# The beta and decay columns of a projection in plain fp32 on four column tiles, and an earlier first norm

## The chip, the cores and the metric

The kernel runs on one core of a Trainium2 chip. The metric is the device time of one execution in microseconds (us), as the median of several runs of the same program. Engine names are those of the profile: PE multiplies matrices, PEld is its weight load, DVE (VectorE), ACT (ScalarE) and POOL (GpSimd) work on vectors, SP (SyncE) issues most transfers.

## What is computed

One layer of a streaming encoder for 320 tokens: 256 of a new stream and 64 of a running one, 2048 channels each.

```python
h = rmsnorm(x, g_pre_mix)
p = h @ w_in                       # 2048 -> 6160 columns
a_out = conformer_conv(p[..., :c0], p[..., c0:c1], ...)          # channels of group A
b_out = gdn_mixer(p[..., c1:c2], p[..., c2:c3],                  # q, k, v and z of group B
                  p[..., c3:c4], p[..., c4:], ...)               # 8 columns for beta, 8 for the decay
x = x + rmsnorm(concat(a_out, b_out) @ w_out, g_post_mix)
x = x + rmsnorm(ffn(rmsnorm(x, g_pre_ffn)), g_post_ffn)

beta = sigmoid(b_raw)
g = -exp(a_log) * softplus(a_raw + dt_bias)
```

`rmsnorm` divides each token by the root of its mean square and multiplies by a weight per channel. The change concerns the last 16 columns of `w_in` (beta and decay, "the gate columns") and the root of the first norm.

## The kernel before

Tokens lie along the free axis (320 elements), channels along the 128 partitions in 16 blocks (`KB`). Each of the large products is done in three matmuls of a rounded type (fp32r): the weight is split into a high and a low part (`whi`, `wlo`, `split_w`, L213-219: a cast on ACT at L217, a subtraction on DVE at L218), and so is the input (`hi_t`, `lo_t`, that is x times the norm's weight g1). Then high by high (L233), high by low (L234) and low by high (L237) are summed in PSUM. The division by the root is done on the result, with `rb`, a row of roots broadcast to all partitions.

**Order at the start.** x and the first weights are loaded; 192 products of four blocks (`FIRST`) go to `ps_first` (L390-400) while ACT and DVE still split the rest. Beside them ACT squares x (`squares`) and DVE sums that into `ssum`, which has two halves of 320 tokens. Then come, in program order, the gate columns (`gate_products`, L307-312: 32 products into `psba`), then a block of `w_in` for v (`in_block(FIRST_V)`, 48 products into `psq`), with the job `first_norm` (L402-405) between them. That job sums `ssum` over partitions with products by a column of ones (`rstd`, L254-266: six matmuls into `pst`, DVE at L264, the power -0.5 on POOL at L265), waits for 36 more products, then turns the roots into a row over all partitions (`rstd_rows`, L268-273: three transposes into `psb`, L272) and ACT copies that to `rb` (L405).

**What sets the order.** `tick` (L148 on) counts the products of the large matmuls. At every 20th (`GAP`) it lets those jobs go one step on that are due; a job is a generator whose `yield` names how many products to wait for and how many PSUM slots it holds. What a job issues comes behind the product at which it was let go. The rest (weights ahead of use, `PRI_W`; urgent steps, `PRI_E`) follows from a priority. A weight goes through three slots `wst` for the loaded block (also used by a block of zeros `zt`) and three of `wsp` for the split. The blocks after `FIRST_V` follow `PLAN` (z blocks, heads h with `qkv_block` L621 on, convolution blocks c).

**The gates.** `gates` (L422-516) copies `psba` on ACT (L424, L425), multiplies by `rb` on DVE (L427, L428), transposes to tokens on partitions in three matmuls into `pst_ba` (L433), copies on ACT (L435) and adds high and low part on DVE (L436). A chain of small DVE operations for the softplus ends in `gt` (L462). 60 products (`LAG_GATE`) later come the sums over tokens, six matmuls into `psg` (L479, L480), then the exponentials and the decay products (`psd`). Between the root and `gt`, DVE also does the short convolutions of q, k and v (`cq`, L632: three steps for each block) and the subtractions of L218. Further on, the head's tail copies `kd` on ACT (L706), and the inverse of small matrices runs on tiles of PE smaller than 128 by 128 (L792, L815, L836).

Of the kernel before, what the change touches and what calls it, by code (L numbers as in the profile page):

```python
# [9 lines left out]
F32 = mybir.dt.float32  # L10
# [7 lines left out]
P = 128  # L18
# [82 lines left out]
def trunk_kernel(ctx, tc, ins, outs):  # L101
# [34 lines left out]
    def start(gen, wait, g=0, t=0):  # L136
        job = [dense[1] + wait, gen, g, t, []]
        jobs.append(job)
        return job
# [8 lines left out]
    def tick(mm):  # L148
        dense[0] = mm.ins
        dense[1] += 1  # L150
        if dense[1] % GAP == 0:
            g, t0, behind, due = 0, held_t[0], dense[0], []
            t = t0
            n0 = len(nc.cur_bb.bb.instructions)
            done = []
            for job in sorted(jobs, key=lambda j: j[0]):
                if job[0] <= dense[1] and g + job[2] <= 4 and t + job[3] <= 2:
                    g += job[2]
                    t += job[3]
                    due.append(job)  # L160
            for job in due:
                if not job[4]:
                    behind = advance(job, behind)
                    done.append(job)
            last_of = [i for x in (mybir.EngineType.Activation, mybir.EngineType.DVE)
                       if (i := newest(x, n0)) is not None]
            for job in due:
                if job[4] and job not in done:
                    with ExitStack() as e:
                        for i in last_of:  # L170
                            e.enter_context(tc.issue_after(i))
                        advance(job)
            held_t[0] = t - t0
            front = newest(mybir.EngineType.DVE, n0)
            for _ in range(min(pace[0], len(taps))):
                next_tap(front)
# [28 lines left out]
    def load_dma(src):  # L205
        w = wst.tile([P, HALF], F32, tag="w", name="w")
        dst = w[:, 0:src.free_size()]
        if len(src.shape) == 3:
            dst = dst.rearrange("p (a f) -> p a f", a=src.shape[1])
        nc.sync.dma_start(dst, src)  # L210
        return w

    def split_w(w, width, pool=None):  # L213
        pool = pool or wsp
        hi = pool.tile([P, HALF], F32R, tag="whi", name="whi")
        lo = pool.tile([P, HALF], F32R, tag="wlo", name="wlo")
        S.copy(hi[:, 0:width], w[:, 0:width])  # L217
        V.tensor_tensor(lo[:, 0:width], w[:, 0:width], hi[:, 0:width].bitcast(F32), ALU.subtract)  # L218
        return hi, lo

    def load_split(src, width, pool=None):
        with tc.high_priority(offset=boost[0]):
            return split_w(load_dma(src), width, pool)

    def block_matmul(ps, src, rhs, nks, final=True, first=True):
        nk = sum(nks)
        k0 = 0
        for nk_part in nks:
            hi, lo = load_split(src[:, k0 * P:(k0 + nk_part) * P], nk_part * P)
            for j in range(nk_part):  # L230
                xh, xl = rhs(k0 + j)
                wh = hi[:, j * P:(j + 1) * P]
                tick(PE.matmul(ps, wh, xh, start=(first and k0 + j == 0), stop=False))  # L233
                tick(PE.matmul(ps, wh, xl, start=False, stop=False))  # L234
            for j in range(nk_part):
                xh, xl = rhs(k0 + j)
                tick(PE.matmul(ps, lo[:, j * P:(j + 1) * P], xh, start=False, stop=(final and k0 + j == nk - 1)))  # L237
            k0 += nk_part
# [68 lines left out]
    def gate_products(wz):  # L307
        psba = ps_p.tile([P, 512], F32, tag="p", name="psba")
        for k in range(KB):
            tick(PE.matmul(psba[:, 0:T], wz[:, k, :], hi_t[k], start=(k == 0), stop=False))  # L310
            tick(PE.matmul(psba[:, 0:T], wz[:, k, :], lo_t[k], start=False, stop=(k == KB - 1)))
        return psba


# [1 line left out]
    with tc.tile_pool(name="xp", bufs=1) as xp:  # L316
# [9 lines left out]
        with tc.high_priority():  # L326
# [6 lines left out]
            nc.sync.dma_start(cst, ins["cst"][:, 0:NCST1])  # L333
            wba = xp.tile([P, KB, 16], F32, tag="wba", name="wba")
            nc.sync.dma_start(wba, ins["w_ba"])
        wbz = xp.tile([P, KB, P], F32R, tag="wbz", name="wbz")
        G.memset(wbz.bitcast(F32), 0.0)
        nc.sync.dma_start(par[:, NGV:NPAR], ins["par"][:, NGV:NPAR])
        nc.sync.dma_start(gpar[:, 0:8], ins["a_log"].partition_broadcast(P))
        nc.sync.dma_start(gpar[:, 8:16], ins["dt_bias"].partition_broadcast(P))  # L340
# [1 line left out]
        with tc.high_priority(offset=PRI_E):  # L342
            keep_warm(psw, NWARM)

            last = {}

            def then(eng, fn, *args, **kw):
                with ExitStack() as e:
                    if eng in last:
                        e.enter_context(tc.issue_after(last[eng].ins))  # L350
                    last[eng] = fn(*args, **kw)

            def split_part(hi, lo, w, o, n):
                then(S, S.copy, hi[:, o:o + n], w[:, o:o + n])
                then(V, V.tensor_tensor, lo[:, o:o + n], w[:, o:o + n], hi[:, o:o + n].bitcast(F32), ALU.subtract)

            ssum = xp.tile([P, 2, T], F32, tag="ssum", name="ssum")

            def squares(k):
                x = xt[k // 4][:, k % 4:k % 4 + 2, :]  # L360
                if k == 0:
                    then(S, S.activation, ssum, x, AF.Square)
                else:
                    sq = xp.tile([P, 2, T], F32, tag="sq", bufs=2, name="sq")
                    then(S, S.activation, sq, x, AF.Square)
                    then(V, V.tensor_tensor, ssum, ssum, sq, ALU.add)

            for k in range(KB):
                x = xt[k // 4][:, k % 4, :]
                g = pv("g1", k)  # L370
                then(S, S.activation, hi_t[k], x, AF.Identity, scale=g)
                then(V, V.scalar_tensor_tensor, lo_t[k], x, g, hi_t[k].bitcast(F32), ALU.mult, ALU.subtract)
                if k % 2 == 0:
                    pre.append((wsp.tile([P, HALF], F32R, tag="whi", name="whi"), wsp.tile([P, HALF], F32R, tag="wlo", name="wlo")))
                if k < 4:
                    split_part(*pre[-1], wg[k // 2], (k % 2) * FW, FW)
                elif k % 2:
                    split_part(*pre[-1], wg[k // 2], 0, 2 * FW)
                if k % 2 and k >= 5:
                    squares(k - 5)  # L380
            then(S, S.copy, wbz[:, :, 0:16], wba)
            then(V, V.tensor_tensor, wbz[:, :, 16:32], wba, wbz[:, :, 0:16].bitcast(F32), ALU.subtract)
            for k in (KB - 4, KB - 2):
                squares(k)
        for i, b in enumerate(FIRST):
            pool = (ps_t, ps_g)[i // 2]
            ready[b] = pool.tile([P, 512], F32, tag=pool.name[-1], name="ps_first")
# [12 lines left out]
                                tick(PE.matmul(ps, w, xl, start=False, stop=False))  # L400

        def first_norm():  # L402
            rr, _ = rstd([ssum[:, 0, :], ssum[:, 1, :]])
            yield 36, 1, 0
            S.copy(rb, rstd_rows(rr)[0])  # L405

        job = start(first_norm(), 24, 1)
        psba = gate_products(wbz)
        ready[FIRST_V] = in_block(FIRST_V, "psq")
        finish(job)  # L410
    boost[0] = PRI_W
    cb = pa.enter_context(tc.tile_pool(name="cb", bufs=2, reuse_waits="tile"))
    gd = pa.enter_context(tc.tile_pool(name="gd", bufs=2, reuse_waits="tile"))
# [2 lines left out]


    gate = {}
    cst2 = act.tile([P, NCST - NCST1], F32, tag="bl7", name="cst2")
    nc.sync.dma_start(cst2, ins["cst"][:, NCST1:NCST])  # L420

    def gates():  # L422
        baT = cb.tile([32, 3, P], F32, tag="un", bufs=1, name="baT").rearrange("p c f -> p (c f)")
        S.copy(baT[:, 0:T], psba[0:32, 0:T])  # L424
        S.copy(baT[:, T:T + TS], psba[0:32, TP:T])  # L425
        yield 1, 0, 0
        V.tensor_tensor(baT[:, 0:T], baT[:, 0:T], rb[0:32, :], ALU.mult)  # L427
        V.tensor_tensor(baT[:, T:T + TS], baT[:, T:T + TS], rb[0:32, TP:T], ALU.mult)  # L428
        ba = const.tile([P, 3, 16], F32, tag="ba", name="ba")
        yield LAG_WAIT, 0, 1  # L430
        pst = ps_t.tile([P, 512], F32, tag="t", name="pst_ba")
        for c in range(3):
            PE.transpose(pst[:, c * 32:(c + 1) * 32], baT[:, c * P:(c + 1) * P], cv("ident", 32, 32))  # L433
        ps3 = pst[:, 0:96].rearrange("p (c f) -> p c f", c=3)
        S.copy(ba, ps3[:, :, 0:16])  # L435
        V.tensor_tensor(ba, ba, ps3[:, :, 16:32], ALU.add)  # L436
        beta = const.tile([P, 3, NH], F32, tag="beta", name="beta")
        S.activation(beta, ba[:, :, 0:8], AF.Tanh, scale=0.5)
        G.tensor_scalar(beta, beta, 0.5, 0.5, ALU.mult, ALU.add)
# [91 lines left out]
    def conv_block(b):  # L531
        psg_ = in_block(8 + b, "psgate")
        ub = ubufs[b % 3]
        with tc.high_priority(offset=PRI_E):
            sg = cb.tile([P, T], F32, tag="sg", bufs=1, name="sg")
            V.tensor_tensor(sg, psg_[:, 0:T], rb, ALU.mult)
            S.activation(sg, sg, AF.Tanh, scale=0.5)
        psv = in_block(b, "psv")
        if b > 2:
            finish_conv(b - 3)  # L540
        with tc.high_priority(offset=PRI_E):
# [782 lines left out]
```

## Time and profile before

| | |
|---|---|
| median of 3 runs | 1489.62 us (1489.47 to 1491.08) |
| the profiled execution | 1489.37 us |
| its span in the profile | 1487.6 us |
| outside the span | 1.8 us |
| granted PE clock | 1.00 |
| first gate product, first `psq` product | 33.96 us, 40.00 us |
| `rb` copied | 45.81 us |
| first `psg` product | 69.05 us |

Times inside the profile are microseconds from the start of its span. A row of the timeline has the start, the duration and the engine, then the line, the operation and its operands (written before read); in square brackets stands the idle time of the engine just before it, and what ended that. A PE product of 320 tokens is listed with 0.31 us or so, but the next one starts 0.15 us behind it: products overlap in the pipeline, so costs are taken from the distance of starts. A plain fp32 product leaves two records, an fp32r product one.

### The profile page before, as it was taken

How to read it: one execution, taken by the hardware profiler on the slowest of the kernel's cores; microseconds unless marked ns; L12 is line 12 of the kernel's file. 1: busy time of each engine (PE TensorE's matmuls, PEld its weight loads, DVE VectorE, ACT ScalarE, POOL GpSimd, SP SyncE). 2: the span in 40 equal slices, each digit the busy share in tenths (PEclk: the TensorE clock that was granted, in tenths of full speed). 3: DMA queues.
4: the chain of work that ended last, by engine and by line, in shares of the span. 5: the costliest groups of instructions: out<-in, count | busy, mean ns of one | idle time of the engine just before them, and what ended most of it. 6: DMA issues, size and time to landing. Idle time of an engine off the chain costs nothing.

```text
span 1487.6 us, 27264 instructions
## 1 busy us (share of the span) xinstructions
PE 1478.6 (99%) x10610; PEld 1458.2 (98%) x10610; DVE 996.6 (67%) x1816; ACT 730.8 (49%) x1331; POOL 230.5 (15%) x390
## 2 busy tenths in 40 slices
PE   9999999999999999999999999999999999999998
PEld 8999999999999989999999999999999999999997
DVE  6779888888989678756336665545666545656554
ACT  7674556655454656544334444334444334444453
POOL 0111101021010000322002322002232001223101
PEclk9999999999999999999999999999999999999999
DMA  8435453544444734444554444554444455444453
GB/s 294 140 115 167 158 151 110 147 156 138 129 122 145 238 128 146 146 156 121 153 168 155 145 154 135 143 162 158 156 143 147 136 148 168 153 156 143 136 148 119
DMA packets 98281, 224.22 MB, mean 151 GB/s; under 512 B 18792, under 2 KB 39528, under 8 KB 98152
## 3 DMA queue, kind: packets, MB, share of 16 engines
q1 hardware_dynamic: 98008, 222.45, 47.8%
q8 instruction: 83, 1.36, 0.4%
q14 instruction: 46, 0.38, 0.1%
q10 hardware_dynamic: 144, 0.03, 0.0%
HBM read 215.33 MB, written 7.12 MB: 150 GB/s over the span
## 4 chain that ended last, share of the span: by engine, by line
PE 95%; ACT 2%; DVE 1%; issue 1%; DMA 0%; POOL 0%; DVEq 0%; ACTq 0%; POOLq 0%
PE psu L237 13%; PE psu L234 13%; PE psu L233 13%; PE psdn L233 7%; PE psdn L234 7%; PE psdn L237 7%; PE psq L233 3%; PE psq L234 3%; PE psq L237 3%; PE psm L237 2%; PE psm L233 2%; PE psm L234 2%; PE psu L1117 1%; PE psv L233 1%; PE psgate L233 1%; PE ps_first L398 1%
## 5 line engine op out<-in xcount | busy, mean ns | idle before, releaser
L217 ACT CAST whi<-w 128x1024 fp32r<-128x1024 f32 (+2 forms) x440 | 412.6, 940 | 488.5 <-PE psu L234 169.7
L218 DVE TENSOR_TENSOR wlo<-w,whi 128x1024 fp32r<-128x1024 f32 (+2 forms) x440 | 477.2, 1085 | 191.4 <-ACT whi L217 123.9
L233 PE MATMUL psu<-hi,whi 128*128 128x320 f32 x1344 | 397.0, 309 | 0.0
L234 PE MATMUL psu<-lo,whi 128*128 128x320 f32 x1344 | 396.9, 309 | 0.0
L234 PEld LDWEIGHTS psu<-lo,whi 128*128 128x128 f32 x1344 | 252.3, 188 | 0.0
L233 PEld LDWEIGHTS psu<-hi,whi 128*128 128x128 f32 x1344 | 252.2, 188 | 0.0
L237 PE MATMUL psu<-hi,wlo 128*128 128x320 f32 x1344 | 224.4, 309 | 0.0
L237 PEld LDWEIGHTS psu<-hi,wlo 128*128 128x128 f32 x1344 | 204.1, 188 | 0.0
L234 PE MATMUL psdn<-gl,whi 128*128 128x320 f32 x660 | 195.9, 310 | 0.0
L1150 POOL COPY nffn<-fbuf 128x2 f32<-128x2 f32 x88 | 99.5, 1131 | 586.7 <-DVE fbuf L1148 583.5
L1148 DVE TENSOR_TENSOR fbuf<-psu,rb 128x256 f32<-128x256 f32 x88 | 37.4, 424 | 169.1 <-PE psu L237 169.0
L233 PE MATMUL psdn<-gh,whi 128*128 128x320 f32 x480 | 142.8, 309 | 0.0
L234 PEld LDWEIGHTS psdn<-gl,whi 128*128 128x128 f32 x660 | 123.9, 188 | 0.3
L233 PE MATMUL psq<-hh,whi 128*128 128x320 f32 x352 | 106.0, 314 | 0.0
L234 PE MATMUL psq<-hl,whi 128*128 128x320 f32 x352 | 104.1, 309 | 0.0
L233 PEld LDWEIGHTS psdn<-gh,whi 128*128 128x128 f32 x480 | 90.1, 188 | 0.0
L237 PE MATMUL psdn<-gh,wlo 128*128 128x320 f32 x480 | 89.9, 309 | 0.0
L237 PEld LDWEIGHTS psdn<-gh,wlo 128*128 128x128 f32 x480 | 75.3, 188 | 0.0
L233 PEld LDWEIGHTS psq<-hh,whi 128*128 128x128 f32 x352 | 66.1, 188 | 0.4
L234 PEld LDWEIGHTS psq<-hl,whi 128*128 128x128 f32 x352 | 66.1, 188 | 0.2
L563 DVE SCALAR_TENSOR_TENSOR cvt<-ub,par,cvt 128x320 f32<-128x320 f32 x120 | 65.3, 545 | 0.1
L1193 DVE TENSOR_TENSOR y<-y,psdn 128x320 f32<-128x320 f32 x45 | 22.0, 488 | 58.7 <-PE psdn L237 58.7
(356 smaller groups left out, 2485.2 us busy)
## 6 DMA issues: line engine op xcount, KB each, us to landing
w<-in_w_up SPq DMA_DIRECT2D x176, 512.0 KB
w<-in_w_in SPq DMA_DIRECT2D x88, 512.0 KB
w<-in_w_down SPq DMA_DIRECT2D x64, 384.0 KB
w<-in_w_down SPq DMA_DIRECT2D x64, 320.0 KB
w<-in_w_out SPq DMA_DIRECT2D x32, 320.0 KB
w<-in_w_out SPq DMA_DIRECT2D x16, 384.0 KB
w<-in_w_first SPq DMA_DIRECT2D x6, 512.0 KB
wtp<-wsp SPq DMA_DIRECT2D x4, 640.0 KB
```

Source lines behind the costliest of these rows:

```text
L217: S.copy(hi[:, 0:width], w[:, 0:width])
L218: V.tensor_tensor(lo[:, 0:width], w[:, 0:width], hi[:, 0:width].bitcast(F32), ALU.subtract)
L233: tick(PE.matmul(ps, wh, xh, start=(first and k0 + j == 0), stop=False))
L234: tick(PE.matmul(ps, wh, xl, start=False, stop=False))
L237: tick(PE.matmul(ps, lo[:, j * P:(j + 1) * P], xh, start=False, stop=(final and k0 + j == nk - 1)))
L398: tick(PE.matmul(ps, w, xh, start=(k == 0 and wt is hi), stop=(k == KB - 1 and wt is lo)))
L563: return lambda: V.scalar_tensor_tensor(acc, x, w, acc, ALU.mult, ALU.add)
L1117: PE.matmul(pss[i][:, 0:T], wt[:, o:o + P], x, start=(k == 0 and n == 0), stop=(k == KB - 1 and n == 2))
L1148: V.tensor_tensor(buf[:, 2:258], psu[:, 0:TP], rb2[:, 0:TP], ALU.mult)
L1150: G.tensor_copy(nffn[:, b, 0, :], buf[:, 256:258])
L1193: V.tensor_tensor(y[:, n, :], y[:, n, :], psd[:, 0:T], ALU.add)
```

## The change

- The gate columns are no longer split. `wbz` holds 32 columns for each block of channels, 16 of them w times g1 (one DVE multiplication), the rest zero; 16 matmuls in plain fp32 take it with x itself. Block k writes to the partitions from 32 (k mod 4) of `psba`: four column tiles, each with the sum of four blocks. Sixteen ticks follow behind the last one.
- DVE adds the two halves of `ssum`, so three matmuls make the sum for the first norm. `first_norm` is due at once, waits 16 products instead of 36, and its second step has a high priority. The next product of a large matmul is issued behind the last `psb` transpose (`pin`).
- The ACT casts of weights are issued behind the copy of `rb` (`hold`) until the first convolution block clears that.
- In `gates` all 128 partitions are copied and multiplied by `rb`; three matmuls by `pick` (four identities of 16 below one another, made by a DVE reduction) add the four tiles and transpose at once. The DVE addition is gone.

```diff
     def split_w(w, width, pool=None):
...
-        S.copy(hi[:, 0:width], w[:, 0:width])
+        with ExitStack() as e:
+            for i in hold:
+                e.enter_context(tc.issue_after(i))
+            S.copy(hi[:, 0:width], w[:, 0:width])
...
-                tick(PE.matmul(ps, wh, xh, start=(first and k0 + j == 0), stop=False))
+                with ExitStack() as e:
+                    if pin:
+                        e.enter_context(tc.issue_after(pin.pop()))
+                    mm = PE.matmul(ps, wh, xh, start=(first and k0 + j == 0), stop=False)
+                tick(mm)
...
         for k in range(KB):
-            tick(PE.matmul(psba[:, 0:T], wz[:, k, :], hi_t[k], start=(k == 0), stop=False))
-            tick(PE.matmul(psba[:, 0:T], wz[:, k, :], lo_t[k], start=False, stop=(k == KB - 1)))
+            i = 32 * (k % 4)
+            mm = PE.matmul(psba[i:i + 32, 0:T], wz[:, k, :], xt[k // 4][:, k % 4, :], start=(k < 4), stop=(k >= KB - 4),
+                           skip_group_check=True)
+        for _ in range(16):
+            tick(mm)
...
-        wbz = xp.tile([P, KB, P], F32R, tag="wbz", name="wbz")
-        G.memset(wbz.bitcast(F32), 0.0)
+        wbz = xp.tile([P, KB, 32], F32, tag="wbz", name="wbz")
+        G.memset(wbz, 0.0)
...
-            then(S, S.copy, wbz[:, :, 0:16], wba)
-            then(V, V.tensor_tensor, wbz[:, :, 16:32], wba, wbz[:, :, 0:16].bitcast(F32), ALU.subtract)
+            then(V, V.tensor_tensor, wbz[:, :, 0:16], wba, pv("g1").unsqueeze(2).to_broadcast((P, KB, 16)), ALU.mult)
             for k in (KB - 4, KB - 2):
                 squares(k)
+            then(V, V.tensor_tensor, ssum[:, 0, :], ssum[:, 0, :], ssum[:, 1, :], ALU.add)
...
-            rr, _ = rstd([ssum[:, 0, :], ssum[:, 1, :]])
-            yield 36, 1, 0
-            S.copy(rb, rstd_rows(rr)[0])
+            rr, _ = rstd([ssum[:, 0, :]])
+            yield 16, 1, 0
+            with tc.high_priority(offset=PRI_E):
+                rows, mm = rstd_rows(rr)
+                pin.append(mm.ins)
+                spread.append(S.copy(rb, rows).ins)
...
-        job = start(first_norm(), 24, 1)
+        spread = []
+        job = start(first_norm(), 0, 1)
...
+    hold.extend(spread)
...
-        baT = cb.tile([32, 3, P], F32, tag="un", bufs=1, name="baT").rearrange("p c f -> p (c f)")
-        S.copy(baT[:, 0:T], psba[0:32, 0:T])
-        S.copy(baT[:, T:T + TS], psba[0:32, TP:T])
+        baT = cb.tile([P, 3, P], F32, tag="un", bufs=1, name="baT").rearrange("p c f -> p (c f)")
+        S.copy(baT[:, 0:T], psba[:, 0:T])
+        S.copy(baT[:, T:T + TS], psba[:, TP:T])
+        V.tensor_reduce(pick, cv("ident").rearrange("p (a j) -> p j a", j=32)[:, 0:16, :], AX.X, ALU.add)
...
-            PE.transpose(pst[:, c * 32:(c + 1) * 32], baT[:, c * P:(c + 1) * P], cv("ident", 32, 32))
-        ps3 = pst[:, 0:96].rearrange("p (c f) -> p c f", c=3)
-        S.copy(ba, ps3[:, :, 0:16])
-        V.tensor_tensor(ba, ba, ps3[:, :, 16:32], ALU.add)
+            PE.matmul(pst[:, c * 16:(c + 1) * 16], baT[:, c * P:(c + 1) * P], pick, start=True, stop=True)
+        S.copy(ba, pst[:, 0:48].rearrange("p (c f) -> p c f", c=3))
...
         psv = in_block(b, "psv")
+        hold.clear()
```

On PE before, this is the end of the gate columns (`psba`), where the sum for the first norm (`pst`) stands among them; `hh` and `hl` are the high and low part of the input, and `psq` is the block for v.

```order
L310 MATMUL psba<-hh_106,wbz 128x320
L311 MATMUL psba<-hl_122,wbz 128x320
L259 MATMUL pst<-cst,ssum 128x1 x6
L310 MATMUL psba<-hh_107,wbz 128x320
L311 MATMUL psba<-hl_123,wbz 128x320
L310 MATMUL psba<-hh_108,wbz 128x320
L311 MATMUL psba<-hl_124,wbz 128x320
L233 MATMUL psq<-hh_93,whi 128x320
L234 MATMUL psq<-hl_109,whi 128x320
```

On PE in the changed kernel, this is the same place; `xt` is the input as it was loaded.

```order
L322 MATMUL psba<-xt_129,wbz 32x320 x4
L322 MATMUL psba<-xt_130,wbz 32x320 x4
L322 MATMUL psba<-xt_131,wbz 32x320 x4
L322 MATMUL psba<-xt_132,wbz 32x320 x4
L270 MATMUL pst<-cst,ssum 128x1 x3
L243 MATMUL psq<-hh_93,whi 128x320
L245 MATMUL psq<-hl_109,whi 128x320
L243 MATMUL psq<-hh_94,whi 128x320
```

The 16 products stand together with the three of the sum behind them; the transposes into `psb` stand behind 12 products of `psq`, where before they stand behind 36. From the `psb` transposes to the `psg` products it is 139 products of 320 tokens, before 154; from the `pst_ba` matmuls to `psg` it is 79, before 114.

On ACT before, these are the casts of weights (`whi`) around the copy of `rb`; the other copies set up buffers and fetch `psba`.

```order
L217 CAST whi<-w 128x1024 x2
L625 COPY qb_593<-par 128x3
L625 COPY qb_594<-par 128x3
L546 COPY ub_587<-par 128x30
L546 COPY ub_588<-par 128x30
L546 COPY ub_589<-par 128x30
L424 COPY baT<-psba 32x320
L425 COPY baT<-psba 32x64
L474 CAST strict<-cst 128x128
L217 CAST whi<-w 128x1024
L405 COPY rb<-psb 128x320
L217 CAST whi<-w 128x1024
```

On ACT in the changed kernel, this is the same place.

```order
L222 CAST whi<-w 128x1024
L645 COPY qb_575<-par 128x3
L645 COPY qb_576<-par 128x3
L566 COPY ub_569<-par 128x30
L566 COPY ub_570<-par 128x30
L566 COPY ub_571<-par 128x30
L444 COPY baT<-psba 128x320
L445 COPY baT<-psba 128x64
L493 CAST strict<-cst 128x128
L422 COPY rb<-psb 128x320
L222 CAST whi<-w 128x1024
L979 ACT_TABLE_LOAD
```

The third and the fourth cast of a weight from `w_in` stood ahead of the copy of `rb`; now the third stands directly behind it, and the fourth behind the first activations that use `rb`.

More of the change, by code (lines that the diff above doesn't have):

```diff
@@ L211, in load_dma @@
         return w
+    hold = []
     def split_w(w, width, pool=None):
@@ L223, in load_split @@
             return split_w(load_dma(src), width, pool)
+    pin = []
     def block_matmul(ps, src, rhs, nks, final=True, first=True):
@@ L418, in trunk_kernel @@
     gate = {}
+    pick = const.tile([P, 16], F32, tag="pick", name="pick")
     cst2 = act.tile([P, NCST - NCST1], F32, tag="bl7", name="cst2")
@@ L422, in gates @@
     def gates():
-        baT = cb.tile([32, 3, P], F32, tag="un", bufs=1, name="baT").rearrange("p c f -> p (c f)")
-        S.copy(baT[:, 0:T], psba[0:32, 0:T])
-        S.copy(baT[:, T:T + TS], psba[0:32, TP:T])
+        baT = cb.tile([P, 3, P], F32, tag="un", bufs=1, name="baT").rearrange("p c f -> p (c f)")
+        S.copy(baT[:, 0:T], psba[:, 0:T])
+        S.copy(baT[:, T:T + TS], psba[:, TP:T])
+        V.tensor_reduce(pick, cv("ident").rearrange("p (a j) -> p j a", j=32)[:, 0:16, :], AX.X, ALU.add)
         yield 1, 0, 0
-        V.tensor_tensor(baT[:, 0:T], baT[:, 0:T], rb[0:32, :], ALU.mult)
-        V.tensor_tensor(baT[:, T:T + TS], baT[:, T:T + TS], rb[0:32, TP:T], ALU.mult)
+        V.tensor_tensor(baT[:, 0:T], baT[:, 0:T], rb, ALU.mult)
+        V.tensor_tensor(baT[:, T:T + TS], baT[:, T:T + TS], rb[:, TP:T], ALU.mult)
         ba = const.tile([P, 3, 16], F32, tag="ba", name="ba")
```

## The prediction

> **What bounds the kernel now.** I read the page first, then the waits of PE, then the timeline of each engine over the first 72 us, where the change acts.
>
> ```profile
> span 1487.6 us, 27264 instructions
> PE 1478.6 (99%) x10610; PEld 1458.2 (98%) x10610; DVE 996.6 (67%) x1816; ACT 730.8 (49%) x1331; POOL 230.5 (15%) x390
> PEclk9999999999999999999999999999999999999999
> ```
>
> PE works 99% of the span, at full clock in every slice. So time goes with PE's own work: what is taken off PE is won, unless PE then waits. The waits of PE say where it does (releaser: total us, times, longest):
>
> ```profile
> PE psm L1063 <- DVE wlo L218: 1.1, 2, 0.8
> PE psz L233 <- ACT whi L217: 0.6, 1, 0.6
> PE psg L479 <- DVE gt L462: 0.2, 1, 0.2
> ```
>
> Two of them lie behind the change: `psg` waits for the gates' chain on DVE, `psz` for a cast on ACT. The third is far on, where the order on PE is the same again. The stretch that is changed, on PE's timeline:
>
> ```profile
> 33.96 0.31 PE L310 MATMUL psba<-hh,wbz 128*128 128x320 f32 x1
> ...
> 37.92 0.31 PE L311 MATMUL psba<-hl,wbz 128*128 128x320 f32 x1
> 38.06 1.40 PE L259 MATMUL pst<-cst,ssum 128*128 128x1 f32 x12
> 39.32 0.39 PE L310 MATMUL psba<-hh,wbz 128*128 128x320 f32 x1
> ```
>
> From the first to the 28th gate product it is 3.96 us over 27 steps: 0.147 us each. The sum for the norm holds PE from 38.06 to 39.32, 1.26 us for 12 records: 0.105 each. Nothing waits here.
>
> **The change, part by part.** *Removed from PE.* 32 products of 0.147 are -4.69 us. Three of six sum matmuls, six records of 0.105, are -0.63. The addition of the halves that replaces them is half of a row such as this one (640 elements in 0.82, so an estimated 0.45 on DVE), and the gate products cover it, since PE needs the sum only at their end:
>
> ```profile
> 31.18 0.82 DVE L351 TENSOR_TENSOR ssum<-ssum,sq 128x640 f32<-128x640 f32 x1
> ```
>
> The multiplication by g1 takes the place of a DVE subtraction of the same size; the ACT cast and most of the memset go. All lie beside the first 192 products: nothing.
>
> *Added to PE: 16 plain fp32 products of 320 tokens.* Plain fp32 at this length stands at the kernel's end; smaller tiles of PE stand in the inverse:
>
> ```profile
> 1476.92 2.33 PE L1239 MATMUL fin<-y,cst 128*128 128x320 f32 x8
> 1479.09 0.43 PE L1160 MATMUL fin<-x,cst 128*128 128x320 f32 x1
> ```
>
> ```profile
> 171.82 0.31 PE L234 MATMUL psgate<-hl,whi 128*128 128x320 f32 x1
> 172.06 0.50 PE L815 MATMUL pz<-wtp,np 32*32 32x32 f32 x20
> 172.50 0.42 PE L233 MATMUL psgate<-hh,whi 128*128 128x320 f32 x1
> 186.29 0.68 PE L836 MATMUL px<-wtp,zq 64*64 64x64 f32 x8
> 160.10 0.53 PE L792 MATMUL pz<-wtp,np 32*32 32x16 f32 x40
> ```
>
> ```profile
> L815 PE MATMUL pz<-wtp,np x80: 191/191/212, 172.1 to 392.8; 32*32 32x32 f32 x80
> L836 PE MATMUL px<-wtp,zq x32: 218/218/267, 186.3 to 407.1; 64*64 64x64 f32 x32
> L792 PE MATMUL pz<-wtp,np x160: 177/178/198, 160.1 to 382.1; 32*32 32x16 f32 x160
> ```
>
> Four products leave eight records in 2.17 us (1476.92 to 1479.09): 0.271 a record, two a product. One after another, 32 records are 8.67 us: dearer than what goes. It hangs on the tiles running side by side. L836 uses one tile at a time: (0.68 - 0.218)/7 = 66 ns a record of 64 columns, half of it 33 for 32. L815 alternates between two tiles: (0.50 - 0.191)/19 = 16.3 ns. So two tiles give 2.0 of 2. L792 takes four tiles in turn, with 16 columns: (0.53 - 0.178)/39 = 9.0 ns where one tile would take 66/4 = 16.5, or 1.8 of 4. Records that short may be held by their issue, not by their columns; 9 ns for each would be no limit to records of 271 ns. No row has four tiles on the same 128 rows. Bounds: 2.17 us four at a time, 8.67 none. I take four at a time, because nothing in the pair of rows makes tiles cost each other anything.
>
> Into and out of the tiles it costs a little: 172.06 - 171.82 is 0.24, 0.09 over a normal step; the group lasts 0.44 (to 172.50), its 20 records 0.33: 0.11. Together 0.20, so 2.35 us. [...]
>
> *The root.* Its chain before:
>
> ```profile
> 39.80 0.87 POOL L265 TENSOR_TENSOR rr<-rr,nhalf 128x3 f32<-128x3 f32 x1 [10.47 <-DVE rr L264]
> 45.29 0.49 PE L272 MATMUL psb<-cst,rr 128*128 128x128 f32 x3
> 45.81 0.43 ACT L405 COPY rb<-psb 128x320 f32<-128x320 f32 x1 [2.21 <-PE psb L272]
> ```
>
> From the end of the sum on PE (39.32) over a step on DVE to the end of POOL (40.67) it is 1.35 us. After: gate products end at 36.3, the sum at 36.94, the root at 38.29; 12 products of `psq` end at 36.94 + 1.76 = 38.70. So 0.4 us of cover, where before it was 4.6 us. If that is gone, the transposes wait by as much, and with them all of PE (the next product is pinned behind them). `rb` then is copied from 39.2 to 39.65, 6.2 us earlier than before; relative to PE's products by 24 of them.
>
> *The held casts.* Before, on ACT and DVE:
>
> ```profile
> 36.20 1.05 ACT L217 CAST whi<-w 128x1024 fp32r<-128x1024 f32 x1 [5.36 <-DMA w<-in_w_in]
> ...
> 46.40 1.05 ACT L217 CAST whi<-w 128x1024 fp32r<-128x1024 f32 x1 [0.16 <-PE psq L234]
> ...
> 50.89 1.04 ACT L217 CAST whi<-w 128x1024 fp32r<-128x1024 f32 x1
> 37.28 1.23 DVE L218 TENSOR_TENSOR wlo<-w,whi 128x1024 fp32r<-128x1024 f32 x1 [4.15 <-ACT whi L217]
> ```
>
> The third cast moves from 36.20 to 39.7-40.75. PE needs it behind 48 products of `psq`, at 36.94 + 7.06 + 0.24 = 44.2: cover 3.4 us. On ACT the table load, zT, qb and cq now stand ahead of the fourth cast. They took from 47.45 to 50.89, 3.44 us: the cast ends at 45.3, needed 24 products on, at 47.75, cover 2.5; its subtraction, behind the short convolutions on DVE, has some 2.0. On SP, transfers queue behind the subtraction that frees their slot, 4.7 us later than before, for products ten and more us away. So nothing; without cover a late cast costs its lateness.
>
> *The gates' chain.* PE's way:
>
> ```profile
> 51.34 0.31 PE L234 MATMUL psq<-hl,whi 128*128 128x320 f32 x1
> 51.58 0.37 PE L433 MATMUL pst_ba<-cst,baT 32*128 32x32 f32 x3
> 51.87 0.41 PE L233 MATMUL psq<-hh,whi 128*128 128x320 f32 x1
> 69.05 0.40 PE L479 MATMUL psg<-gt,cst 128*128 128x16 f32 x2 [0.19 <-DVE gt L462]
> 69.29 0.37 PE L480 MATMUL psg<-gt,cst 128*128 128x8 f32 x2
> ```
>
> The three transposes cost 0.53 - 0.15 = 0.38. The three plain fp32 matmuls have six records: 0.63 by the sum's row, 0.72 by two `psg` records in 0.24. I take +0.25. `psg` stands 154 products behind `psb` before, 139 after: 15 x 0.147 = 2.20 us less time for DVE, 1.95 with those 0.25. What DVE loses in that stretch is three `cq` steps and the addition; its busy time there (PE, PEld, DVE, ACT, POOL) shows how full it is:
>
> ```profile
> 46.27:68.99 22.72, 22.59 (x154) 22.09 (x152) 20.53 (x50) 18.35 (x43) 1.89 (x3) 1.00 0.41 140
> 50.37 2.87 DVE L632 SCALAR_TENSOR_TENSOR cq<-qb,par,cq 128x320 f32<-128x320 f32 x6 [0.76 <-ACT cq L630]
> 53.56 0.20 DVE L436 TENSOR_TENSOR ba<-ba,pst_ba 128x48 f32<-128x48 f32 x1
> ```
>
> Three `cq` of 2.87/6 = 0.48 are 1.43, the addition 0.11 to the next start: 1.54. So `psg` comes 1.95 earlier and `gt` 1.54: the wait grows from 0.2 to some 0.6. DVE idles 22.72 - 20.53 = 2.19 us of the stretch, part of which can be used up. I take +0.3; bounds -0.35 (wait gone) and +2.5 (none of DVE's time is won).
>
> *The cast before psz.*
>
> ```profile
> 102.62 0.37 ACT L706 ACTIVATE kd<-tkq,sc 128x128 f32<-128x128 f32 x1 [1.14 <-POOL sc L699]
> 107.02 0.37 ACT L706 ACTIVATE kd<-tkq,sc 128x128 f32<-128x128 f32 x1 [0.69 <-POOL sc L699]
> 109.59 2.93 ACT L217 CAST whi<-w 128x1024 fp32r<-128x1024 f32 x3
> 110.68 0.41 PE L233 MATMUL psz<-hh,whi 128*128 128x320 f32 x1 [0.58 <-ACT whi L217]
> ```
>
> The second tail's transposes, which start the `kd` copies ahead of that cast, now stand 40 products ahead of `psz`, not 56: 2.35 us less slack. Against it, work of ACT moves ahead of them and fills its waits (1.14 + 0.69), and PE's copies come sooner. I take 0, bounds -0.74 (the whole gap ahead of it) and +2.35.
>
> *Sum:* -4.69 - 0.63 + 2.35 + 0.25 + 0.3 + 0 = -2.42 us. The profiled execution took 1489.37 (span 1487.6 and 1.8 around it), 0.25 under the median of 1489.62. So 1486.95 by the one, **1487.2 us** by the other, -0.16%: under the 0.2% (2.98 us) that a measurement of this kernel can tell from no change.
>
> **The rivals.** *Two at a time.* If the two records of a product stay together on their tile and products start in order, only the second record of one meets the first of the next. Then 16 x 0.271 + 0.20 = 4.54 us, the sum is -0.23, and the time 1489.4. For it speaks L792 with 1.8 of 4; against it L815, whose 2.0 of 2 such an order allows as well, though no more. *One after another, slower.* If tiles on the same 128 rows share what feeds those rows, 32 records take 8.67 + 0.20: +4.10 us, 1493.7. Each tile in L815 has rows of its own, so the trace doesn't exclude it. It decides from 7.7 us on for the 16 products (2.98 + 4.69 + 0.63 - 0.25 - 0.3). *The gates' chain late.* DVE wins none of its time, `psg` waits 2.5 us: -0.22, 1489.4. Against it the three steps less ahead of `gt`; for it that subtractions of weights, held back to the same stretch, stand among the chain's steps.
>
> **How the numbers follow.** Four at a time 0.66, two 0.17, one 0.11, the late chain 0.06. Within the first, both waits gone (-0.65 and -0.74 on the sum) gives 1485.8; a little under that, 1485.5, is the low end. The high end, 1490.6, takes in the second and fourth with the upper half of the `psz` bound; outside are the third and the tails. Faster by over 0.2% (under 1486.6) is some two fifths of the likeliest case: 0.28. Slower (over 1492.6): the third and a sum of late chain and late cast, 0.13. Within: 0.59.
>
> **What would show it.** Right: the gate products' records start some 0.068 us apart and the stage lasts 2.3 to 2.8 us; `psb` starts near 38.7 and `rb` is copied near 39.2; `psg` waits for `gt` by 0.3 to 0.8; no wait of PE for a weight between 37 and 60 us. Wrong: a gate stage of 4.5 or 8.9 us; a wait at `psb` for POOL; waits for `wlo` ahead of 60 us; `psz` waiting over 1 us.

## The result and the profile after

The changed kernel takes 1492.85 us (median of 21 runs, 1490.36 to 1495.6), the kernel before 1489.62 (21 runs, 1488.54 to 1491.08): a ratio of 1.0021, 95% interval 1.0015 to 1.0027. It is slower by some 3.2 us, where 2.4 us less were forecast. The profiled execution has a span of 1491.2 us, 3.6 over that of before. The page's head:

```profile
span 1491.2 us, 27264 instructions
PE 1478.5 (99%) x10607; PEld 1455.1 (98%) x10607; DVE 997.7 (67%) x1817; ACT 730.6 (49%) x1330; POOL 234.1 (16%) x390
```

PE is busy for as long as before, although work of 3 us was taken from it. Either a product takes longer somewhere, or PE stands idle: here it is both. The main waits of PE that were not there before or have grown:

```profile
PE pvns L913 <- DVE rhs L905: 1.1, 1, 1.1
PE px L842 <- ACT zq L837: 0.9, 1, 0.9
PE psg L498 <- DVE gt L481: 0.9, 1, 0.9
PE psz L243 <- ACT whi L222: 0.8, 1, 0.8
PE px L818 <- ACT zh L813: 0.5, 1, 0.5
```

`px`, `pvns` and their like belong to the heads' inverse and delta rule, 80 us and more behind the lines that were edited. To see where the time goes, the start of the same product was taken from the PE records of each trace, at the first product of a block, in us from the start of that trace's span. The rows name the block and its start in the kernel before; the columns are differences to that (the kernels of the later columns are the experiments below):

```
block   before   changed  16 ticks  psg     32 ticks  32 t.,   32 t.,     32 t.,
        at us    kernel   less      later             zeros    exp first  psg later
psq      40.00   -2.80    +0.05     -2.83   -2.73     -2.84    -3.18      -3.20
psgate   70.78   +0.17    +0.02     -2.56   +3.32     +2.27    -2.99      -4.74
psq      86.25   -0.30    +0.01     -3.03   +3.58     +1.79    -2.99      -3.40
psz     110.68   -0.06    +0.25     -2.79   +3.56     +1.77    -2.99      -3.42
psq     184.44   -1.14    -0.82     -3.87   +3.56     +1.77    -2.98      -3.42
psq     257.36   +1.26    +1.67     -1.30   +3.56     +1.76    -2.99      -3.42
psm     409.97   +4.01    +4.44     +1.47   +3.57     +1.78    -2.99      -3.40
psy     769.58   +3.59    +5.74     +1.22   +3.94     +1.96    -3.00      -4.44
```

Read the column of the changed kernel downwards. At 40 us it is 2.80 ahead, at 71 us it is not: 3 us are lost in between. From 86 to 410 us another 4.3 are lost. From there on little more happens.

**The start is as forecast.** On PE's timeline, the gate products, the sum, the first `psq` product and the transposes:

```profile
34.22 2.36 PE L322 MATMUL psba<-xt,wbz 128*32 128x320 f32 x32
36.51 0.83 PE L270 MATMUL pst<-cst,ssum 128*128 128x1 f32 x6
37.20 0.40 PE L243 MATMUL psq<-hh,whi 128*128 128x320 f32 x1
...
39.05 0.49 PE L283 MATMUL psb<-cst,rr 128*128 128x128 f32 x3
```

From the first gate product to the sum it is 2.29 us, for 32 records that would take 8.67 one after another: four tiles do run side by side. The transposes follow 12 products of `psq` without a wait.

**The first loss: a wait, and a slower clock behind it.** PE's timeline around `psg`:

```profile
61.47 0.39 PE L498 MATMUL psg<-gt,cst 128*128 128x16 f32 x2 [0.87 <-DVE gt L481]
...
65.01 0.47 PE L243 MATMUL psq<-hh,whi 128*128 128x320 f32 x1
65.28 0.47 PE L245 MATMUL psq<-hl,whi 128*128 128x320 f32 x1
...
66.96 0.31 PE L243 MATMUL psq<-hh,whi 128*128 128x320 f32 x1
67.11 0.31 PE L245 MATMUL psq<-hl,whi 128*128 128x320 f32 x1
```

PE waits 0.87 us for `gt` (before 0.19). Then products start 0.27 apart (65.01, 65.28) where it is 0.15 before and behind (66.96, 67.11). The windows view gives the granted clock in its last column but two:

```profile
62.00:63.00 1.00, 1.00 (x10) 1.00 (x9) 1.00 (x3) 0.98 (x2) 0.00 (x0) 0.83 0.00 0
63.00:64.00 1.00, 1.00 (x5) 1.00 (x6) 1.00 (x4) 0.78 (x4) 0.31 (x1) 0.50 0.40 127
64.00:65.00 1.00, 1.00 (x5) 1.00 (x5) 1.00 (x3) 0.00 (x0) 1.00 (x2) 0.50 0.89 340
65.00:66.00 1.00, 1.00 (x5) 1.00 (x5) 1.00 (x3) 0.22 (x1) 1.00 (x1) 0.50 0.15 57
66.00:67.00 1.00, 1.00 (x9) 1.00 (x8) 0.44 (x1) 0.92 (x2) 0.70 (x2) 0.97 0.00 0
```

The clock is at half from 62.66 to 66.07. These 3.4 us cost 1.7 us on top of the wait, and PE counts as busy all the while. Before, the clock was 1.00 here.

Why `gt` is late shows on ACT: the exponential of the softplus (`ex`) stands behind a cast that waits for a weight. In the changed kernel:

```profile
52.06 1.05 ACT L222 CAST whi<-w 128x1024 fp32r<-128x1024 f32 x1 [1.39 <-DMA w<-in_w_in]
...
54.88 0.22 ACT L466 ACTIVATE ex<-na 128x24 f32<-128x24 f32 x1
```

In the kernel before, the cast ahead of it waits for PE, not for its weight:

```profile
57.45 1.06 ACT L217 CAST whi<-w 128x1024 fp32r<-128x1024 f32 x1 [1.01 <-PE psq L234]
...
61.37 0.22 ACT L447 ACTIVATE ex<-na 128x24 f32<-128x24 f32 x1
```

And why the weight is late shows on DVE and in SP's queue: the load can be issued only when the subtraction three weights earlier has freed its slot. That subtraction, of the fourth weight, and SP's next load:

```profile
47.05 1.22 DVE L223 TENSOR_TENSOR wlo<-w,whi 128x1024 fp32r<-128x1024 f32 x1
48.30 0.33 SPq L210 DMA_DIRECT2D w<-in_w_in  x1
```

The same two in the kernel before:

```profile
43.78 1.23 DVE L218 TENSOR_TENSOR wlo<-w,whi 128x1024 fp32r<-128x1024 f32 x1 [4.12 <-PE psq L237]
45.03 0.34 SPq L210 DMA_DIRECT2D w<-in_w_in  x1
```

The load starts 3.3 us later, although PE is 2.8 us ahead: 6 us of lead are gone. For the changed kernel itself this chain is read from the trace; the experiments below test it in the kernel ticks_32.

**The second loss** lies in the order of DVE and ACT. Around 195 us, in the kernel before, DVE and then PE:

```profile
192.85 0.35 DVE L885 SCALAR_TENSOR_TENSOR rhs<-ks,neG,vh 64x128 f32<-64x128 f32 x1
...
193.70 0.36 DVE L885 SCALAR_TENSOR_TENSOR rhs<-ks,neG,vh 64x128 f32<-64x128 f32 x1
...
196.00 1.22 DVE L218 TENSOR_TENSOR wlo<-w,whi 128x1024 fp32r<-128x1024 f32 x1
```

```profile
195.06 0.39 PE L893 MATMUL pvns<-rhs,wtp 128*128 128x128 f32 x2
```

In the changed kernel:

```profile
195.66 1.22 DVE L223 TENSOR_TENSOR wlo<-w,whi 128x1024 fp32r<-128x1024 f32 x1
...
197.25 0.34 DVE L905 SCALAR_TENSOR_TENSOR rhs<-ks,neG,vh 64x128 f32<-64x128 f32 x1
...
198.09 0.36 DVE L905 SCALAR_TENSOR_TENSOR rhs<-ks,neG,vh 64x128 f32<-64x128 f32 x1
```

```profile
198.59 0.46 PE L913 MATMUL pvns<-rhs,wtp 128*128 128x128 f32 x2 [1.08 <-DVE rhs L905]
```

The two `rhs` steps stood well ahead of a weight's subtraction; now they stand behind it and behind a convolution step, and PE waits for them. Nothing there was edited. Of the 4.3 us from 86 to 410 us, 3.0 are idle time of PE (`pvns` 1.08, `px` 1.51, `psz` 0.26 more than before); the rest is spread over many small products. But the job steps go by a count of products, one step at each 20th. The changed kernel counts 16 products fewer at the gate columns, so each later step of a job falls on another place among the blocks: 16 products later for the first inverse (`pz`, at the 752nd product behind the gate columns instead of the 736th), 4 earlier for somewhat more than half of all.

### The profile page after: what moved, and what is told of

The parts are those of the page before. It is cut to its first block, busy times and chain, and to the rows that moved or that the text cites. A ratio compares the mean times of both kernels' runs of the same rounds, so it can differ in the third digit from the quotient of the medians.

```text
span 1491.2 us, 27264 instructions
## 1 busy us (share of the span) xinstructions
PE 1478.5 (99%) x10607; PEld 1455.1 (98%) x10607; DVE 997.7 (67%) x1817; ACT 730.6 (49%) x1330; POOL 234.1 (16%) x390
## 4 chain that ended last, share of the span: by engine, by line
PE 85%; DVE 7%; ACT 3%; DMA 2%; issue 2%; POOL 1%; SPq 0%; ACTq 0%; DVEq 0%; POOLq 0%
PE psu L248 13%; PE psu L243 13%; PE psu L245 13%; PE psdn L243 7%; PE psdn L245 7%; PE psdn L248 6%; DVE wlo L223 2%; PE psq L243 2%; PE psq L245 2%; PE psq L248 2%; PE psm L248 2%; PE psm L243 2%; PE psm L245 2%; PE psu L1137 1%; ACT whi L222 1%
```

## The experiments

The theory after this reading: the start won what was forecast; `psg` lost 2.4 us of it (0.7 by the wait, 1.7 by the clock), since the held casts delay a weight that ACT waits for; the shifted count lost the rest. The rivals are named with each run.

**psg_later.** The changed kernel with

```diff
-        yield LAG_GATE, 1, 0
+        yield 100, 1, 0
...
-            yield LAG_DECAY, 1, 0
+            lags.append(0)
+            yield (10 if len(lags) == 1 else 10 if len(lags) == 2 else LAG_DECAY), 1, 0
```

> The changed kernel with the psg products 21 products further on (at 172 behind the gate columns, not 151); the first two decay products follow sooner, so that everything behind them stands where the change has it. Theory (an idle PE at psg lowers its clock, and the later order costs the rest): no wait at psg, granted clock 1.00 from 60 to 72 us, about 0.7 us of wait and 1.6 us of half clock less: 1490.6 us. Rival (the lower clock has nothing to do with that wait): only the wait goes, 1492.2 us, and the clock still falls near 63 us.

Measured: 1491.05 us (ratio to before 1.0009, interval 1.0000 to 1.0017). No wait at `psg`, and the clock is 1.00 in every stretch from 30 to 110 us (mean of the profiled execution 1.000). The table has -2.56 at 71 us where the changed kernel has +0.17: 2.7 us, of which the wait explains 0.9. What is left of the loss comes behind 184 us, from -3.87 to +1.47. The theory holds: without the first loss, the kernel is still no faster than before.

**wait_filled.** The changed kernel with

```diff
-        yield LAG_GATE, 1, 0
+        yield 80, 1, 0
         psg = ps_g.tile([P, 512], F32, tag="g", name="psg")
+        for _ in range(4):
+            PE.matmul(psg, wz[:, 0:P], wz, start=True, stop=True)
```

and the first `LAG_DECAY` set to 10, so that later steps stay.

> The changed kernel with four products of zeros (128x512) on PE directly ahead of psg, one product later than the change has psg: PE works where it waited. Theory (the idle PE lowers the clock): granted clock 1.00 from 60 to 72 us, 1.6 us less: 1491.2 us. Rival (the clock falls by itself there, or because of the small psg products): clock still near 0.5 for some 3 us, 1492.9 us.

PE's timeline and the windows of this kernel:

```profile
60.49 1.04 PE L498 MATMUL psg<-wz 128*128 128x512 bf16 x4
61.45 0.39 PE L501 MATMUL psg<-gt,cst 128*128 128x16 f32 x2
```

```profile
62.00:64.00 2.00, 2.00 (x17) 2.00 (x17) 2.00 (x5) 1.74 (x5) 0.33 (x1) 1.00 0.21 49
64.00:66.00 2.00, 2.00 (x15) 2.00 (x14) 2.00 (x5) 1.14 (x2) 2.00 (x2) 1.00 0.54 213
```

`psg` starts at 61.45 as in the changed kernel (61.47), with the same small products behind it, but the clock stays at 1.00, and the block at 70.78 comes 1.56 us early instead of 0.17 late. So in this trace neither the place nor the small products alone lower the clock: with PE at work where it waited, it stays at 1.00. The whole kernel took 1492.51 us (1.0016, interval 1.0008 to 1.0025), 0.3 under the changed kernel and not the 1.6 expected; the intervals overlap. Its profile loses 4.8 us behind 86 us where the changed kernel loses 3.9. And the changed kernel's 21 runs have a mean clock from 0.998 to 1.000, so its clock does not fall by as much each time. Its seven runs at 0.998 have a median of 1493.13 us, the seven at 1.000 one of 1492.19, still 2.6 over the kernel before. The slower clock is thus a part of the loss, and not the larger one; what it costs on average is not settled by this pair.

**before_16_ticks.** The kernel before with

```diff
-            tick(PE.matmul(psba[:, 0:T], wz[:, k, :], lo_t[k], start=False, stop=(k == KB - 1)))
+            PE.matmul(psba[:, 0:T], wz[:, k, :], lo_t[k], start=False, stop=(k == KB - 1))
...
-        job = start(first_norm(), 24, 1)
+        job = start(first_norm(), 4, 1)
```

> The kernel before, where only the first of each two gate products is counted: 16 ticks less, so that all later job steps stand where the changed kernel has them; nothing else of the change. Theory (the later order alone costs what was lost behind 72 us, 3.9 us by the two profiles): 1493.5 us. Rival (the later order is neutral, the loss hangs on held weights or on the earlier start): 1489.6 us.

Measured: 1494.77 us (1.0031, interval 1.0019 to 1.0043). No product was added. Its waits of PE hold the changed kernel's new ones:

```profile
PE pvns L893 <- DVE rhs L885: 1.2, 1, 1.2
...
PE px L822 <- ACT zq L817: 0.9, 1, 0.9
PE psz L233 <- ACT whi L217: 0.8, 1, 0.8
PE px L798 <- ACT zh L793: 0.5, 1, 0.5
```

In the table its column falls and rises with that of the changed kernel from 110 us on (+0.25 and -0.06, -0.82 and -1.14, +1.67 and +1.26, +4.44 and +4.01), and the clock is 1.00 all along (mean of the profiled execution 1.000). The count alone costs over 4 us up to the end of these blocks; 1.3 more come later, at other waits.

**ticks_32.** The changed kernel with

```diff
-        for _ in range(16):
+        for _ in range(32):
             tick(mm)
...
-            yield 16, 1, 0
+            yield 36, 1, 0
```

> The changed kernel with 32 ticks behind the gate products instead of 16, and the first norm's second step after 36 counted products (24 of psq): every later job step stands behind the same product as in the kernel before, and psg 155 products behind psb, as before 154. Theory: no wait at psg, no new waits later, all of the start's gain kept: 1487.0 us. Rival (the held weights or the earlier start cost the later loss, whatever the order): 1489.5 us or more.

Measured: 1489.99 us (1.0001, interval 0.9992 to 1.0010), runs from 1486.79 to 1493.27; the profiled one is the slowest of these. The later order is right again: the table stays between +3.56 and +3.58 from 86 to 410 us, so nothing is lost there. But between 40 and 71 us six are, against the theory, which had no wait at `psg`:

```profile
67.91 0.39 PE L498 MATMUL psg<-gt,cst 128*128 128x16 f32 x2 [3.15 <-DVE gt L481]
```

```profile
55.70 1.05 ACT L222 CAST whi<-w 128x1024 fp32r<-128x1024 f32 x1 [3.22 <-DMA w<-in_w_in]
...
59.17 0.23 ACT L466 ACTIVATE ex<-na 128x24 f32<-128x24 f32 x1
```

```profile
68.00:70.00 2.00, 2.00 (x13) 2.00 (x14) 1.87 (x4) 1.56 (x5) 0.00 (x0) 0.72 0.54 182
...
75.00:76.00 1.00, 1.00 (x6) 1.00 (x5) 1.00 (x3) 0.66 (x3) 0.00 (x0) 0.65 0.00 0
```

The distance from `psb` to `psg` (155 products) was not the point: the cast ahead of `ex` waits 3.2 us for its weight, `psg` 3.15 us for `gt`, and the clock is at half for 6.8 us. The two runs with a mean clock of 1.000 took 1486.79 and 1487.32 us, what the theory expected; so the loss differs from run to run, and this trace shows it at its largest. The rival on the held weights was right about the place. The next runs ask by which way.

**ticks_32_zeros.** The kernel of ticks_32 with

```diff
-    zt = wst.tile([P, HALF], F32, tag="w", name="zt")
-    G.memset(zt, 0.0)
+    zeros = wz.bitcast(F32)[:, 0:P].unsqueeze(1)
...
-                              zt[:, 0:(a1 - a0) * P].rearrange("p (a f) -> p a f", f=128))
+                              zeros.to_broadcast((P, a1 - a0, P)))
```

> The kernel of ticks_32, where the block of zeros no longer takes one of the three slots of loaded weights (its transfers read zeros that are there already), so that SP need not wait for them ahead of the next weight. Theory (the gates' chain is late since the exponential of the softplus stands on ACT behind a cast that waits for a late weight): that cast no longer waits 3.2 us, psg waits under 0.5 us, clock 1.00, 1487.0 us. Rival (DVE's own order makes gt late): the cast comes earlier, but psg waits as before; 1490 us.

Measured: 1490.63 us (1.0007, interval 0.9998 to 1.0015). The cast still waits, and PE still waits 3.0 us for `gt`:

```profile
55.47 1.05 ACT L222 CAST whi<-w 128x1024 fp32r<-128x1024 f32 x1 [3.10 <-DMA w<-in_w_in]
```

So the slot of the zeros was not what made the weight late. As read above, its load is issued behind a subtraction (at 50.02 us here, 50.11 in ticks_32). But the transfer is slower too: from that issue to the cast it takes 5.5 us (5.6 in ticks_32), in the changed kernel 3.8. Why, no run asks.

**ticks_32_exp_first.** The kernel of ticks_32 with the steps from the softplus's argument to its exponential at high priority, `psg` at 176 and the decay products as close behind it as keeps the later order:

```diff
+        with tc.high_priority(offset=PRI_E):
-        V.tensor_tensor(ax, ba[:, :, 8:16], dtb, ALU.add)
+            V.tensor_tensor(ax, ba[:, :, 8:16], dtb, ALU.add)
...
-        S.activation(ex, na, AF.Exp)
+            S.activation(ex, na, AF.Exp)
...
-        yield LAG_GATE, 1, 0
+        yield 100, 1, 0
```

> The kernel of ticks_32, where ACT takes the exponential of the softplus ahead of the cast that waits for a late weight, and DVE its neighbours early; psg nearly where ticks_32 has it (at 176 instead of 179), everything behind the decay products in its place. Theory (gt is late since that exponential stands behind the waiting cast): gt comes 3 us or more earlier against PE, psg waits under 0.3 us, clock 1.00: 1486.5 us. Rival (DVE is full, so gt is late by its subtractions and convolutions whatever ACT does): psg still waits 2 us or more, 1490 us.

Measured: 1486.94 us (0.9979, interval 0.9970 to 0.9988). ACT, DVE and PE:

```profile
53.45 0.22 ACT L468 ACTIVATE ex<-na 128x24 f32<-128x24 f32 x1
54.42 1.05 ACT L222 CAST whi<-w 128x1024 fp32r<-128x1024 f32 x1 [0.74 <-DMA w<-in_w_in]
```

```profile
63.77 0.18 DVE L483 SCALAR_TENSOR_TENSOR gt<-pl,ea 128x24 f32<-128x24 f32 x1
```

```profile
64.01 0.39 PE L500 MATMUL psg<-gt,cst 128*128 128x16 f32 x2
```

The exponential stands ahead of the waiting cast, at 53.45 instead of 59.17, and PE waits only 0.12 us at `psg`. The column in the table is flat at -3.0 from 71 us to the end: what the start won is kept. `psg` stands three products earlier than in ticks_32, so DVE had less time and not more. The order of these small steps decided. Of the 5.7 us that `ex` won, 2.4 are DVE's (`na`, which it reads, ends at 52.0 instead of 54.4), the rest is the place on ACT. The theory holds in this form.

**ticks_32_psg_later.** The kernel of ticks_32 with `yield 140, 1, 0` for the gates and the first four `LAG_DECAY` set to 10.

> The kernel of ticks_32 with psg 37 products further on (at 216), the decay products closer behind it, everything after them in its place. Theory (the wait at psg and the low clock behind it are all that was left of the loss): no wait there, clock 1.00, 1487.0 us. Rival (late weights cost PE elsewhere too): 1489 us or more.

Measured: 1485.92 us (0.9974, interval 0.9963 to 0.9985; 7 runs from 1484.90 to 1486.28), faster than both kernels. The cast still waits 2.38 us for its weight, but nobody waits for `gt` (at 66.38; `psg` starts at 69.56). So a cast that waits for its weight need not cost PE anything.

**norm_alone.** The kernel before with the change's first norm and its held casts, but the old gate columns:

```diff
-            rr, _ = rstd([ssum[:, 0, :], ssum[:, 1, :]])
-            yield 36, 1, 0
-            S.copy(rb, rstd_rows(rr)[0])
+            rr, _ = rstd([ssum[:, 0, :]])
+            yield 16, 1, 0
+            with tc.high_priority(offset=PRI_E):
+                rows, mm = rstd_rows(rr)
+                pin.append(mm.ins)
+                spread.append(S.copy(rb, rows).ins)
```

> The kernel before with the change's first norm alone (one sum, earlier second step, the pinned product and the held casts); the gate columns as before, and the later order as before. Its gain on PE is three sum matmuls, 0.6 us. Theory (the held casts make weights late, and with them the exponential and gt): the cast ahead of the exponential waits for its transfer, psg waits 1 to 2 us and the clock falls: 1491 us. Rival (without the shorter gate columns there is time enough): no new wait, 1489.0 us.

Measured: 1488.02 us (0.9988, interval 0.9980 to 0.9997). The theory expected too much: the cast ahead of `ex` waits 0.66 us for its weight, `psg` 0.36 for `gt`, and the clock stays at 1.00 (mean of the profiled execution 1.000). `psg` stands 165 products behind `psb` here, not 139 as in the changed kernel. The held casts alone are harmless; that they do harm together with a PE that comes to `psg` 3 us sooner is inferred. No run has the changed kernel without them.

**before_8_more, before_12_more.** The kernel before with 8 or 12 more ticks behind the gate columns.

```diff
-            tick(PE.matmul(psba[:, 0:T], wz[:, k, :], lo_t[k], start=False, stop=(k == KB - 1)))
+            mm = PE.matmul(psba[:, 0:T], wz[:, k, :], lo_t[k], start=False, stop=(k == KB - 1))
+            tick(mm)
+        for _ in range(12):
+            tick(mm)
         return psba
```

> The kernel before with 12 more ticks behind the gate columns: every later job step stands 8 products earlier or 12 later against the blocks than in the kernel before. Theory (the order behind was fitted to one phase of the count, and any other costs): slower by 2 to 6 us, 1492 to 1495 us. Rival (only the phase of the changed kernel is bad): 1489.5 us.

> The kernel before with 8 more ticks behind the gate columns: later job steps 12 products earlier or 8 later against the blocks. Theory (any other phase costs): slower by 2 to 6 us. Rival (only the phase of the changed kernel is bad): 1489.5 us.

In the traces the two are exchanged: with 12 more the later steps stand 12 products earlier or 8 later, with 8 more 8 earlier or 12 later.

Measured: 1499.65 us with 12 (1.0062, interval 1.0049 to 1.0076) and 1494.48 with 8 (1.0030, interval 1.0018 to 1.0042). With 12 PE waits three times for the inverse:

```profile
PE px L801 <- ACT zh L796: 4.8, 3, 2.3
PE psz L233 <- ACT whi L217: 1.7, 1, 1.7
```

Of four phases of the count that were run in the kernel before (0, 4, 8 and 12 more; 16 less is the same as 4 more), the given one is the fastest by over 4 us. With 12 it loses 9.9 us, where 2 to 6 were expected; its four runs have a mean clock of 0.997 or 0.998, those of the kernel before beside them 0.999 or 1.000.

**tiles_in_turn.** The changed kernel with

```diff
-            i = 32 * (k % 4)
-            mm = PE.matmul(psba[i:i + 32, 0:T], wz[:, k, :], xt[k // 4][:, k % 4, :], start=(k < 4), stop=(k >= KB - 4),
+            i = 32 * (k // 4)
+            mm = PE.matmul(psba[i:i + 32, 0:T], wz[:, k, :], xt[k // 4][:, k % 4, :], start=(k % 4 == 0), stop=(k % 4 == 3),
```

> The changed kernel with the 16 gate products in another order over the same four tiles: four in a row on one tile, then four on the next. Theory (only neighbours on different tiles run side by side): 32 records of 0.271 one after another, with an overlap at three borders: 8 to 8.7 us where it was 2.3. Rival (the tiles keep queues of their own, or narrow products are cheaper): 2.3 to 4.5 us.

```profile
33.70 5.66 PE L322 MATMUL psba<-xt,wbz 128*32 128x320 f32 x32
```

Measured: 5.6 us for the stage (one run, 1498.27 us in all), between the two. The starts of the records show why 8 was too much: first four records come alone, 0.27 us apart, then twelve pairs, then four alone again. So twelve records start beside another one, where the theory had one at each of three borders; 20 starts of 0.27 us are 5.4 us. In the changed kernel the records start in groups of four, 5 to 8 ns apart within a group, and a group comes every 0.27 us. Why the records pair as they do here, no run asks.

## Why the prediction was wrong

The forecast was 2.4 us less, and 3.2 us more were measured. The parts at the start came out; what failed are three things behind them that were put at nothing or nearly so. In the order of the sum:

- *Gate columns, sum, root:* right. The stage was put at 2.35 us and took 2.29. The gain from the first gate product to the first of `psq` was put at 2.97 and is 3.06 (6.04 us before, 2.98 after); 2.80 of it are left in the table, since the gate columns start 0.26 us later. The two rivals on the tiles (two at a time, one after another) are out. `psb` follows without a wait, as forecast.
- *The held casts:* "So nothing" was the failed step for what hangs on them. PE's own need of the third and fourth weight was covered. But the working stopped at "products ten and more us away": the weight loaded into the freed slot is cast on ACT well before PE needs it, and ACT came to the gates' exponential only behind that cast (54.88 us behind 52.06).
- *The gates' chain:* the wait at `psg` was put at 0.5 us and was 0.87, inside its bounds and a little over the 0.3 to 0.8 that were named as a sign of being right. What was missing is that a wait of PE may cost more than its length. Each wait was priced as idle time alone; here half clock followed, which cost 1.7 us. Against the 0.68 more wait that is the larger term.
- *psz:* put at 0; the column goes from -0.30 to -0.06 there, so 0.24 was lost. The wait is 0.83, before 0.58.
- *The later order:* no term at all. The first part of the prediction put the waits far on aside with "where the order on PE is the same again". Between `psz` and that place lie 300 us in which each job step stands elsewhere, and it costs some 4 us (psg_later: from -2.79 to +1.47; before_16_ticks: from +0.25 to +4.44). This is the largest error, and it decides the sign. It could have been seen: 32 counted products became 16, and the difference of 16 is not a multiple of 20. None of the signs that the prediction named lies behind `psz`, so nearly all of its signs of being right came true, and none of being wrong.

With the count and the gates' chain repaired, the forecast of the parts was near: ticks_32_exp_first is at -3.0 us in its profile and 1486.94 us, where 1487.2 was forecast for the change.

What stays open: how often the wait at `psg` lowers the clock, why one of 0.87 us there lowers it and one of 1.08 us at `pvns` does not, why the transfer of the late weight takes 5.6 us in ticks_32 and 3.8 in the changed kernel, and whether the changed kernel without the held casts would wait at `psg`.

## What to carry to other kernels

Where a scheduler releases work by a count, a change in the number of counted steps moves all that is released later; keep the count the same (here: 32 ticks for 16 products) and test the change apart from it. When work is delayed, follow not only who needs its result but also whose buffer it frees, and what stands behind the consumer of the next load in the order of its engine. On a kernel bound by PE, price a new wait by what the clock does behind it too.

## What the runs showed of the hardware

- The granted clock fell to 0.50 for 3.41 us (62.66 to 66.07) behind a wait of 0.87 us at `psg` in the changed kernel, 1.2 us after the first product there; for 3.4 us behind one of 0.73 us in tiles_in_turn, and for 6.8 us behind one of 3.15 us in ticks_32. Behind a wait of 1.85 us at `pvns` in tiles_in_turn, products started 0.27 us apart (203.51 to 205.37 us), as they do at half clock. Behind one of 1.08 us there in the changed kernel the clock stayed at 1.00 (199.19 to 202.60 us). It stayed at 1.00 behind waits of 0.19 (before) and 0.36 us (norm_alone) at `psg`, and when four products of zeros filled the 0.87 (60 to 68 us in wait_filled).
- The idle time of PE does not tell these two apart: of the 3.42 us ahead of the fall in the changed kernel (59.24 to 62.66) PE was busy for 2.55, of 3.42 us with the wait at `pvns` (195.77 to 199.19), behind which the clock did not fall, for 2.34. What does tell them apart is not shown.
- Plain fp32 products on four column tiles over the same 128 rows ran four at a time (2.29 us for 32 records of 0.271), with no loss against a quarter of 8.67 beyond some 0.1 us.
- In tiles_in_turn the same 32 records took 5.6 us: four started alone, then twelve pairs, then four alone, each 0.27 us behind the one before. The trace does not name which record of a product is which.
